# A hybrid decoder step on one core: the first row half's squares summed on VectorE, and query blocks without the learned rows' columns

## The chip, the cores and the metric

The kernel runs on one core of a Trainium2 chip. Its engines are TensorE (PE for its matmuls, PEld for its weight loads), VectorE (DVE), ScalarE (ACT), GpSimd (POOL) and SyncE (SP), whose queue issues most DMAs. The metric is the device time of one execution in microseconds. Lower is better.

## The reference, cut to what matters

512 prompt tokens, 8 sample tokens and 16 learned rows (meta tokens) of width 2048 pass through one layer: an input layer norm, one input projection (queries, keys, values, pool input), windowed attention and a multi-scale pooling side by side, an output projection, a layer norm, a gated feed-forward part of width 5632, and a layer norm. The learned rows stand at the front of the prompt as keys and values, and are dropped from the result. In short:

```python
h   = layer_norm(concat([meta, x]), ln_in_g, ln_in_b)
z   = h @ w_in + b_in                       # -> q | k | v | u
q,k = partial_rope(q, pos), partial_rope(k, pos)
mix = concat([window_attention(q, k, v, sinks), pool_mixer(u)]) @ w_o
h1  = layer_norm(alpha * h + mix, ln1_g, ln1_b)     # mean, mean of squared deviations
y   = layer_norm(alpha * h1 + (silu(h1 @ w_gate) * (h1 @ w_up)) @ w_down, ln2_g, ln2_b)
```

There is one layer, so nothing after the attention reads what the learned rows' own queries would give. All data are fp32.

## The kernel before, in words

Everything is held transposed: features on the 128 partitions, tokens along the free dimension. There are 536 columns: 16 learned rows (META), 8 sample tokens, 512 prompt tokens. They are worked on in two halves: in the input projection 276 columns (the learned rows and 260 tokens) and 260 columns; behind it, where the learned rows are gone, 260 and 260 (HN).

A product of fp32 accuracy is made of three single-pass products. `split` (lines 185 and 186) makes of a weight quarter of 512 columns a high half on ACT (a rounding copy) and a low half on DVE (the rest), into a ring of a few buffers; `products` (lines 201, 202, 204) then multiplies high by high, high by low and low by high. A block of 128 output features is `full_block`: 16 K tiles, in four quarters, each with three matmuls for each column half. The plain 32-bit matmuls (the mean, the variance, the products ahead) show as two instructions each.

The order of the work: input layer norm and keys and values (to about 90 us); eight query blocks (`q_block`) and eight pool blocks (`u_block`), interleaved with the attention of each query block by an explicit order on PE (to about 350 us); `out_proj(0)` for the first 260 columns, `out_proj(1)` for the second; then the layer norm of the second half with fourteen products computed ahead on plain 32-bit matmuls (to about 602 us); the gate and up products by a Strassen-Winograd scheme in 22 turns (to about 1490 us); the down products; the last layer norm.

`ln1(h, zs)` is the layer norm behind the output projection, a generator. For the first half it runs as the side of `out_proj(1)`: after each of the 16 feature blocks of that projection (each about 5.8 us of PE) one more piece of it is put into the program. Its steps: the mean by a matmul with a matrix of 1/2048; for each of eight pairs of K tiles (520 columns side by side) a subtraction of the mean on DVE (line 877), a square on ACT (line 879), and in `var` (line 873) two plain matmuls with the matrix of 1/2048 that add the pair's squares into one bank, which at the end holds the variance in all partitions. `rstd_of` (lines 234 to 240) makes the reciprocal root; then line 891 multiplies and line 894 scales, and `put` (856, 857) splits the result. The squares lie in a ring "t" of three buffers (NT), which also serves the loads of the residual (`hb`) and others; another ring "fill" of five (NF) is for the results of products computed ahead.

Inside these explicit orders, a planner places the instructions of each engine at build time by a simulated clock, by readiness and program order; the loads and splits of weights have a raised priority. Each engine then runs its list strictly in that order.

Of the kernel before, what the change touches and what calls it, by code (L numbers as in the profile page):

```python
# [7 lines left out]
F32 = mybir.dt.float32  # L8
F32R = mybir.dt.float32r
AF = mybir.ActivationFunctionType  # L10
# [3 lines left out]
P = 128  # L14
# [3 lines left out]
META = 16  # L18
# [5 lines left out]
HN = NTOK // 2  # L24
XN = META + HN
XH = [slice(0, XN), slice(XN, C_ALL)]
# [12 lines left out]
NF = 5  # L39
# [13 lines left out]
PG, PB, PBIAS, PSC, PG1, PB1, PSINK, PSS, NPAR = 0, 16, 32, 52, 60, 76, 92, 108, 110  # L53
# [13 lines left out]
def hybrid_step(ctx, tc, xin, w_in, w_o, w_g, w_u, w_d, w_pool, par_d, cst_d, ident_d, ln2gb, kct_d, vc_d, hist_d,  # L67
                ck_d, cv_d, sp_d, yp, ys, nkp, nvp, npp, nks, nvs, nps):
    nc = tc.nc
# [69 lines left out]
    par = cp.tile([P, NPAR], F32, name="par")  # L139
    onesd = cp.tile([P, P], F32, name="onesd")  # L140
# [34 lines left out]
    def load_raw(src, name):  # L175
        raw = wp.tile([P, 1024], F32, tag="raw", name=f"raw_{name}", bufs=NRAW)[:, :src.shape[-1]]
        with tc.high_priority(prio[0]):
            nc.sync.dma_start(raw, src)
        return raw

    def split(s, name, lo=None):

        wh, wl = [sp[0].tile(list(s.shape), F32R, tag=t, bufs=sp[1]) for t in ("wh", "wl")]
        with tc.high_priority(prio[0]):
            nc.scalar.copy(wh, s)  # L185
            last_lo[0] = (lo or nc.vector).tensor_sub(wl, s, wh.bitcast(F32)).ins  # L186
        return wh, wl
# [10 lines left out]
    def products(out, wh, wl, hi, lo, first, last, onto=False):  # L198

        for j, o in enumerate(out):  # L200
            nc.tensor.matmul(o, wh, hi[j], start=first, stop=False, skip_group_check=onto)  # L201
            nc.tensor.matmul(o, wh, lo[j], start=False, stop=False, skip_group_check=onto)  # L202
        for j, o in enumerate(out):
            nc.tensor.matmul(o, wl, hi[j], start=False, stop=last, skip_group_check=onto)  # L204

    def full_block(src, name, out, hi, lo, low=None, apart=False):


        def mm(w, g, js):
            for kk in range(4):  # L210
                k = g * 4 + kk
                sl = slice(kk * P, (kk + 1) * P)
                products([out[j] for j in js], w[0][:, sl], w[1][:, sl], [hi(k)[j] for j in js], [lo(k)[j] for j in js],
                         k == 0, k == KT - 1)

        js = list(range(len(out)))
        ws = []
        for h in range(2):
            raw = load_raw(src[:, h * 1024:(h + 1) * 1024], f"{name}_{h}")
            for g in range(2):  # L220
                ws.append(split(raw[:, g * 512:(g + 1) * 512], f"{name}_{h}{g}", low))
                mm(ws[-1], 2 * h + g, js[:1] if apart else js)
        if apart:
            for g in range(4):
                mm(ws[g], g, js[1:])
# [27 lines left out]
    with ExitStack() as sa:  # L253
# [3 lines left out]
        def mm_tile(name):  # L257
            return ps.tile([P, 512], F32, tag="mm", name=name, bufs=2)
# [4 lines left out]
        def zt_tile(name, n=C_ALL):  # L263
            return pa.tile([P, 2 * XN], F32, tag="zt", name=name, bufs=4)[:, :n]
# [80 lines left out]
        xw = [x.stop - x.start for x in XH]  # L345
        xhi = [act.tile([P, KT, xw[h]], F32R, name=f"xhi{h}") for h in range(2)]
        xlo = [act.tile([P, KT, xw[h]], F32R, name=f"xlo{h}") for h in range(2)]
# [32 lines left out]
                y = y[:, :, META:]  # L380
            last.append(nc.sync.dma_start(h_d[ks, :, HALF[h]].rearrange("k p c -> p k c"), y).ins)

        def in_block(i, name, halves=(0, 1), low=None, apart=False):
            out = [mm_tile(f"mm_{name}_{h}")[:, :xw[h]] for h in halves]
            full_block(w_in[i], name, out, lambda k: [xhi[h][:, k, :] for h in halves],
                       lambda k: [xlo[h][:, k, :] for h in halves], low, apart)
            return out

        def rope(z, dst, name):
            zs = zt_tile(f"zs_{name}")  # L390
            nc.vector.stream_shuffle(zs, z, SWAP)
            nc.vector.tensor_mul(zs, zs, rs)
            nc.vector.tensor_mul(z, z, rc)
            nc.vector.tensor_add(dst, z, zs)


        kT = pa.tile([P, 2, C_ALL], F32, name="kT")
# [16 lines left out]
        def kv_banks(h):  # L414
            return [mm_tile(f"kv{i}_{h}")[:, :xw[h]] for i in range(2)] + \
                   [aux_tile([P, 512], "sc", f"kv{i}_{h}", 4)[:, :xw[h]] for i in (2, 3)]
# [15 lines left out]
        out = kv_banks(0)  # L432
# [4 lines left out]
        for h in range(2):  # L437
# [27 lines left out]
            with step(*three):  # L465
                for i in range(4):
                    nc.scalar.activation(zkv[i][:, XH[h]], out[i], AF.Identity, bias=par[:, PBIAS + i:PBIAS + i + 1])
                if h == 0:
                    out = kv_banks(1)
                    x_split(1, 0)  # L470
        cst = pa.tile([P, NCST], F32, name="cst")
        rc, rs = cst[:, CC:CC + C_ALL], cst[:, CS:CS + C_ALL]
# [16 lines left out]
        for i in range(2):  # L489
            z = zkv[2 + i]  # L490
# [22 lines left out]
        nc.gpsimd.memset(qd, 0.0)  # L513

        def q_block(t):
            out = in_block(4 + t, f"q{t}")
            z = zt_tile(f"zq{t}")
            for h, o in enumerate(out):
                nc.vector.tensor_scalar(z[:, XH[h]], o, par[:, PBIAS + 4 + t:PBIAS + 5 + t], 0.125,
                                        op0=ALU.add, op1=ALU.mult)  # L520
            q = pa.tile([P, C_ALL], F32, tag="q", name=f"q{t}", bufs=3)
            rope(z, q, f"q{t}")
            for j in range(2):
                h = slice(64 * j, 64 * j + 64)
                nc.vector.tensor_copy(qd[h, j, t, :], q[h, C_S:C_P])
            return q
# [275 lines left out]
    pb, gp = Pool(fr), Pool(rr, Region("mid_b", F32R, MDW))  # L802
# [3 lines left out]
    def bank(name, w=HN):  # L806
        return ps.tile([P, 512], F32, tag="bank", name=name, bufs=banks)[:, :w]
# [17 lines left out]
    def pair(d, k2, h):  # L825
        return d[2 * k2:2 * k2 + 2, :, HALF[h]].rearrange("k p c -> p k c")

    def t_tile(name):
        return pb.tile([P, 2, HN], F32, tag="t", name=name, bufs=NT)
# [24 lines left out]
    def put(name, i, s):  # L854
        hi, lo = bop[name][i]
        nc.scalar.copy(hi, s)
        nc.vector.tensor_sub(lo, s, hi.bitcast(F32))

    def ln1(h, zs):


        mp = bank(f"mean{h}")
        nc.tensor.matmul(mp, onesd, zs, start=True, stop=True)
        mean = pb.tile([P, HN], F32, tag="zs", bufs=2)
        nc.scalar.copy(mean, mp)
        yield
        vp = bank(f"var{h}")
        both = lambda x: x.rearrange("p (a b) -> p a b", a=1).to_broadcast([P, 2, HN])
        sqs = []

        def var(k2):
            for j in range(2):
                nc.tensor.matmul(vp, onesd, sqs[k2][:, j, :], start=(k2 + j == 0), stop=(k2 + j == 8))

        for k2 in range(8):
            a = z1[h][k2]
            nc.vector.tensor_sub(a, a, both(mean))
            sqs.append(t_tile(f"sq{h}_{k2}"))
            nc.scalar.activation(sqs[k2], a, AF.Square)
            if k2:  # L880
                var(k2 - 1)
            if k2 % 2 and h == 0:
                yield
        var(7)
        with tc.high_priority(LP):
            r = rstd_of(pb, vp, P, f"ln1{h}")
        yield

        def norm(k2):
            a = z1[h][k2]  # L890
            nc.vector.tensor_mul(a, a, both(r))
            for j in range(2):
                k = 2 * k2 + j
                nc.scalar.activation(a[:, j, :], a[:, j, :], AF.Identity, scale=par[:, PG1 + k:PG1 + k + 1],
                                     bias=par[:, PB1 + k:PB1 + k + 1])
            nc.sync.dma_start(pair(h1_d, k2, h), a)
            return a

        if h == 0:
            for k2 in range(8):  # L900
                put("b11" if k2 < 4 else "b21", k2 % 4, norm(k2))
                yield
            return
        for i in range(4):
            c11, c21, c12 = z1[0][i], z1[0][i + 4], norm(i)
            c22 = norm(i + 4)
            yield

            t1, t2 = t_tile(f"t1_{i}"), t_tile(f"t2_{i}")
            nc.vector.tensor_sub(t1, c12, c11)  # L910
            nc.vector.tensor_sub(t2, c22, t1)
            put("t2", i, t2)
            put("t1", i, t1)
            yield
            t3, t4 = t_tile(f"t3_{i}"), t_tile(f"t4_{i}")
            nc.vector.tensor_sub(t3, c22, c12)
            put("t3", i, t3)
            nc.vector.tensor_sub(t4, c21, t2)
            put("t4", i, t4)
            put("b22", i, c22)  # L920
            yield
# [119 lines left out]
    def staged(go, i):  # L1041
# [17 lines left out]
        for n, y in ((1, go[1]), (3, t12), (5, t34)):  # L1059
# [6 lines left out]
            yield  # L1066

    g0 = ln1(0, out_proj(0))
    zs1 = out_proj(1, g0)
    for _ in g0:  # L1070
# [7 lines left out]
    for j, s in enumerate(sets[NKEEP:NKEEP + NFILL]):  # L1078
        if j % 2 == 0:
            f = pb.tile([P, 2, HN], F32, tag="fill", name=f"fill{j}", bufs=NF)  # L1080
# [27 lines left out]
    accp, rp, pb = Pool(fr), Pool(fr), Pool(fr)  # L1108
    low = fr.take(4 * 1280)
# [94 lines left out]
    for x, (c, j) in enumerate(pairs[2:], 2):  # L1204
# [5 lines left out]
        for i in range(5):  # L1210
# [7 lines left out]
            elif j == 0 and i == 0:  # L1218

                ah, al_ = [], []  # L1220
                for f in range(2 * len(PLAIN)):
                    t = slot(f"af{f}", (NTOK,), 16 + f).bitcast(F32)
# [19 lines left out]
    pb, zp = Pool(fr), Pool(Region("mid_c", F32, MDW))  # L1242
# [153 lines left out]
```

## Time and profile before

| | us |
|---|---|
| three runs | 1973.35, 1977.85, 1978.29 (median 1977.85) |
| the profiled execution | 1976.38, its span 1974.6 |
| busy in the span: PE, DVE, ACT | 1916.5, 1545.2, 936.6 |
| mean granted TensorE clock | 0.987 |

An engine's busy time is the union of its instructions' durations. PE's instructions overlap each other: a new one starts before the one ahead has ended, so the distance from start to start is what one costs in a dense stream. DMA is busy for about half of its capacity, and moves 162 GB/s over the span.

### The profile page before, as it was taken

What the parts mean: (1) busy time and instruction counts of PE and PEld (TensorE: products, weight loads), DVE (VectorE), ACT (ScalarE), POOL (GpSimd) and SP (SyncE); (2) the same over time, 40 slices, a digit from 0 to 9 for tenths busy, and PEclk for the clock granted to TensorE, in tenths of its full rate; (3) what the DMA queues carried; (4) which work ended last, traced back from release to release, by engine and by line L of the source; (5) the groups of instructions that cost most, each with busy time, mean ns of one, the idle gap of its engine ahead of it and who ended that gap; (6) DMA issues with size and microseconds to landing.
All of it is one profiled execution on the core that took longest, in us unless ns stands there. A gap on an engine that the chain in (4) does not pass through costs nothing.

```text
span 1974.6 us, 39350 instructions
## 1 busy us (share of the span) xinstructions
PE 1916.5 (97%) x15571; PEld 1881.8 (95%) x15571; DVE 1545.2 (78%) x2730; ACT 936.6 (47%) x1805; POOL 2.5 (0%) x8
## 2 busy tenths in 40 slices
PE   8999999999999999999999999999999999999995
PEld 8999999999988888999999999999999999999995
DVE  6665657766776878788888888888777888888878
ACT  6644445545654434455554545555545434344331
POOL 0000000000000000000000000000000000000000
PEclk9999999999999999999999999999999999999997
DMA  8732222665744453545445453545549664645332
GB/s 264 231 101 67 67 81 71 216 201 170 247 151 145 136 174 125 171 136 167 145 140 162 148 169 125 169 143 169 176 173 365 209 223 166 223 168 202 86 97 87
DMA packets 144984, 319.25 MB, mean 162 GB/s; under 512 B 14160, under 2 KB 65944, under 8 KB 144696
## 3 DMA queue, kind: packets, MB, share of 16 engines
q1 hardware_dynamic: 143680, 314.65, 48.2%
q8 instruction: 122, 2.00, 0.4%
q10 hardware_dynamic: 1120, 2.10, 0.3%
q14 instruction: 62, 0.51, 0.1%
HBM read 265.20 MB, written 54.03 MB: 162 GB/s over the span
## 4 chain that ended last, share of the span: by engine, by line
PE 58%; DVE 5%; DMA 2%; issue 1%; ACT 1%; DVEq 0%; ACTq 0%; SPq 0%
PE tri L201 7%; PE tri L204 7%; PE tri L202 7%; PE p_u L201 6%; PE p_u L202 6%; PE p_u L204 6%; PE p_g L201 6%; PE p_g L204 6%; PE p_g L202 6%; DMA fr<-in_w_g_dram 2%; DVE fr L194 2%; DVE rr L186 1%; PE d L204 1%; DMA t_d<-fr 1%; PE d L202 1%
## 5 line engine op out<-in xcount | busy, mean ns | idle before, releaser
L185 ACT CAST rr<-fr 128x512 fp32r<-128x512 f32 (+1 forms) x1056 | 655.6, 643 | 849.7 <-DVE fr L194 289.0
L186 DVE TENSOR_TENSOR rr<-fr,rr 128x512 fp32r<-128x512 f32 (+1 forms) x1056 | 733.4, 716 | 265.6 <-ACT rr L185 253.7
L194 DVE TENSOR_TENSOR fr<-fr 128x1024 f32<-128x1024 f32 (+1 forms) x304 | 319.3, 1050 | 37.3 <-DMA fr<-in_w_g_dram 21.7
L201 PE MATMUL p_g<-rr 128*128 128x260 f32 x800 | 231.2, 290 | 15.9 <-DVE fr L999 6.7
L204 PE MATMUL p_g<-rr 128*128 128x260 f32 x800 | 225.8, 287 | 1.1 <-DVE rr L186 1.1
L201 PE MATMUL p_u<-rr 128*128 128x260 f32 x800 | 225.5, 283 | 0.0
L204 PE MATMUL p_u<-rr 128*128 128x260 f32 x800 | 222.0, 282 | 0.0
L202 PE MATMUL p_g<-rr 128*128 128x260 f32 x768 | 219.6, 287 | 0.0
L202 PE MATMUL p_u<-rr 128*128 128x260 f32 x768 | 216.0, 282 | 0.0
L204 PE MATMUL tri<-rr 128*128 128x260 f32 x696 | 196.8, 283 | 1.2 <-DVE rr L186 1.2
L201 PE MATMUL tri<-rr 128*128 128x260 f32 x696 | 197.1, 283 | 0.8 <-ACT rr L185 0.8
L202 PE MATMUL tri<-rr 128*128 128x260 f32 x696 | 196.7, 283 | 0.0
L201 PEld LDWEIGHTS p_g<-rr 128*128 128x128 f32 x800 | 154.2, 193 | 19.9 <-DVE fr L999 7.7
L204 PEld LDWEIGHTS p_g<-rr 128*128 128x128 f32 x800 | 153.3, 193 | 1.4 <-DVE rr L186 1.3
L201 PEld LDWEIGHTS p_u<-rr 128*128 128x128 f32 x800 | 150.6, 188 | 0.0
L204 PEld LDWEIGHTS p_u<-rr 128*128 128x128 f32 x800 | 149.7, 189 | 0.0
L202 PEld LDWEIGHTS p_g<-rr 128*128 128x128 f32 x768 | 148.0, 193 | 0.0
L201 PE MATMUL o<-rr 128*128 128x260 f32 x512 | 146.0, 286 | 0.3 <-ACT rr L185 0.3
L202 PEld LDWEIGHTS p_u<-rr 128*128 128x128 f32 x768 | 144.3, 188 | 0.0
L204 PE MATMUL o<-rr 128*128 128x260 f32 x512 | 143.9, 283 | 0.2 <-DVE rr L186 0.2
L202 PE MATMUL o<-rr 128*128 128x260 f32 x512 | 144.0, 282 | 0.0
L204 PEld LDWEIGHTS tri<-rr 128*128 128x128 f32 x696 | 131.3, 189 | 1.7 <-DVE rr L186 1.4
(299 smaller groups left out, 4591.5 us busy)
## 6 DMA issues: line engine op xcount, KB each, us to landing
fr<-in_w_g_dram SPq DMA_DIRECT2D x95, 512.0 KB
fr<-in_w_u_dram SPq DMA_DIRECT2D x95, 512.0 KB
fr<-in_w_d_dram SPq DMA_DIRECT2D x64, 640.0 KB
t_d<-fr SPq DMA_DIRECT2D x140, 260.0 KB
fr<-in_w_o_dram SPq DMA_DIRECT2D x64, 512.0 KB
fr<-in_w_in_dram SPq DMA_DIRECT2D x46, 512.0 KB
rr<-t_d SPq DMA_DIRECT2D x87, 260.0 KB
mid_b<-t_d SPq DMA_DIRECT2D x53, 260.0 KB
```

Of the source, the lines that this page charges most:

```text
L185: nc.scalar.copy(wh, s)
L186: last_lo[0] = (lo or nc.vector).tensor_sub(wl, s, wh.bitcast(F32)).ins
L194: i = op(*args).ins
L201: nc.tensor.matmul(o, wh, hi[j], start=first, stop=False, skip_group_check=onto)
L202: nc.tensor.matmul(o, wh, lo[j], start=False, stop=False, skip_group_check=onto)
L204: nc.tensor.matmul(o, wl, hi[j], start=False, stop=last, skip_group_check=onto)
```

## The change

Two things. First, the query blocks compute only the 520 columns of tokens, not those of the 16 learned rows: the first column half of a query block's matmuls goes from 276 to 260 columns, and the steps behind it (bias and scale, rotation) are made on 520 instead of 536. Pool blocks are as before.

Second, in the layer norm of the first row half the eight pairs' squares are no longer sent to PE one by one. DVE adds them up into one buffer `ss`, which takes the first place of the ring "fill", and two plain matmuls over that sum stand in for sixteen. The pieces of the generator (where it yields) are the same. The second row half is as before.

```diff
-        def in_block(i, name, halves=(0, 1), low=None, apart=False):
-            out = [mm_tile(f"mm_{name}_{h}")[:, :xw[h]] for h in halves]
-            full_block(w_in[i], name, out, lambda k: [xhi[h][:, k, :] for h in halves],
-                       lambda k: [xlo[h][:, k, :] for h in halves], low, apart)
+        def in_block(i, name, c0=0, apart=False):
+
+            halves, cs = (0, 1), (slice(c0, xw[0]), slice(0, xw[1]))
+            out = [mm_tile(f"mm_{name}_{h}")[:, cs[h]] for h in halves]
+            full_block(w_in[i], name, out, lambda k: [xhi[h][:, k, cs[h]] for h in halves],
+                       lambda k: [xlo[h][:, k, cs[h]] for h in halves], apart=apart)
...
-        def rope(z, dst, name):
-            zs = zt_tile(f"zs_{name}")
+        def rope(z, dst, name, c0=0):
+            zs = zt_tile(f"zs_{name}")[:, c0:]
+            z = z[:, c0:]
             nc.vector.stream_shuffle(zs, z, SWAP)
-            nc.vector.tensor_mul(zs, zs, rs)
-            nc.vector.tensor_mul(z, z, rc)
-            nc.vector.tensor_add(dst, z, zs)
+            nc.vector.tensor_mul(zs, zs, rs[:, c0:])
+            nc.vector.tensor_mul(z, z, rc[:, c0:])
+            nc.vector.tensor_add(dst[:, c0:], z, zs)
...
-            out = in_block(4 + t, f"q{t}")
+            out = in_block(4 + t, f"q{t}", META)
...
-                nc.vector.tensor_scalar(z[:, XH[h]], o, par[:, PBIAS + 4 + t:PBIAS + 5 + t], 0.125,
+                nc.vector.tensor_scalar(z[:, (slice(META, XN), XH[1])[h]], o, par[:, PBIAS + 4 + t:PBIAS + 5 + t], 0.125,
...
-            rope(z, q, f"q{t}")
+            rope(z, q, f"q{t}", META)
...
             nc.vector.tensor_sub(a, a, both(mean))
+            if h == 0:
+
+                if k2 == 0:
+                    ss = pb.tile([P, 2, HN], F32, tag="fill", name="ss", bufs=NF)
+                    nc.scalar.activation(ss, a, AF.Square)
+                else:
+                    sq = t_tile(f"sq{h}_{k2}")
+                    nc.scalar.activation(sq, a, AF.Square)
+                    nc.vector.tensor_add(ss, ss, sq)
+                if k2 % 2:
+                    yield
+                continue
             sqs.append(t_tile(f"sq{h}_{k2}"))
             nc.scalar.activation(sqs[k2], a, AF.Square)
             if k2:
                 var(k2 - 1)
-            if k2 % 2 and h == 0:
-                yield
-        var(7)
+        if h == 0:
+            for j in range(2):
+                nc.tensor.matmul(vp, onesd, ss[:, j, :], start=(j == 0), stop=(j == 1))
+        else:
+            var(7)
```

## Rows read from the trace of the kernel before

**Rows 1.** The page: busy time by engine, and the granted clock in 40 slices.
```profile
PE 1916.5 (97%) x15571; PEld 1881.8 (95%) x15571; DVE 1545.2 (78%) x2730; ACT 936.6 (47%) x1805; POOL 2.5 (0%) x8
PEclk9999999999999999999999999999999999999997
```

**Rows 2.** What PE waited for from 100 to 560 us: total, times, longest.
```profile
PE o L201 <- ACT rr L185: 0.3, 1, 0.3
```

**Rows 3.** By stretch: length, busy PE, PEld, DVE, ACT, POOL; granted clock; DMA.
```profile
100.00:150.00 50.00, 50.00 (x421) 48.08 (x421) 33.11 (x106) 20.97 (x58) 0.00 (x0) 1.00 0.29 96
300.00:310.00 10.00, 10.00 (x66) 9.57 (x63) 8.89 (x38) 5.29 (x22) 0.00 (x0) 0.72 0.49 153
451.00:487.00 36.00, 36.00 (x275) 35.00 (x274) 22.50 (x40) 18.13 (x31) 0.00 (x0) 1.00 0.51 162
```

**Rows 4.** PE in order of time (start, us, instruction) in a query block.
```profile
150.72 0.29 PE L201 MATMUL mm_q<-rr 128*128 128x276 f32 x1
150.85 0.29 PE L202 MATMUL mm_q<-rr 128*128 128x276 f32 x1
150.98 0.29 PE L201 MATMUL mm_q<-rr 128*128 128x260 f32 x1
151.10 0.28 PE L202 MATMUL mm_q<-rr 128*128 128x260 f32 x1
...
155.18 0.29 PE L201 MATMUL mm_q<-rr 128*128 128x276 f32 x1
```

**Rows 5.** PE in order of time in the output projection of the second half.
```profile
488.31 0.28 PE L204 MATMUL o<-rr 128*128 128x260 f32 x1
...
495.51 0.28 PE L204 MATMUL o<-rr 128*128 128x260 f32 x1
```

**Rows 6.** PE in order of time around one pair of the variance, and later.
```profile
456.85 0.28 PE L204 MATMUL o<-rr 128*128 128x260 f32 x1
456.97 1.04 PE L873 MATMUL var<-fr 128*128 128x260 f32 x4
...
457.97 0.28 PE L202 MATMUL o<-rr 128*128 128x260 f32 x1
...
460.65 0.28 PE L204 MATMUL o<-rr 128*128 128x260 f32 x1
```

**Rows 7.** DVE, then ACT, in order of time, with idle time ahead and its releaser.
```profile
452.25 4.96 DVE L877 TENSOR_TENSOR fr<-fr 128x520 f32<-128x520 f32 x8
457.13 1.89 DVE L186 TENSOR_TENSOR rr<-fr,rr 128x512 fp32r<-128x512 f32 x3
...
462.58 0.69 DVE L186 TENSOR_TENSOR rr<-fr,rr 128x512 fp32r<-128x512 f32 x1 [1.68 <-ACT rr L185]
...
452.74 0.62 ACT L185 CAST rr<-fr 128x512 fp32r<-128x512 f32 x1 [0.94 <-PE o L202]
...
458.10 0.64 ACT L879 ACTIVATE fr<-fr 128x520 f32<-128x520 f32 x1 [0.39 <-PE var L873]
```

**Rows 8.** DVE from 452 to 512 us, one group: busy us, mean ns, idle.
```profile
L891 DVE TENSOR_TENSOR fr<-fr 128x520 f32<-128x520 f32 x8 | 5.0, 692 | 0.0
```

**Rows 9.** PE in order of time: a wait; around the products computed ahead.
```profile
508.30 0.39 PE L204 MATMUL o<-rr 128*128 128x260 f32 x1 [0.22 <-DVE rr L186]
...
545.69 1.92 PE L963 MATMUL p_g<-fr 128*128 128x260 f32 x8
...
602.45 0.48 PE L201 MATMUL p_g<-mid_b,rr 128*128 128x260 f32 x1
```

**Rows 10.** What PE waited for from 600 to 1400 us: total, times, longest.
```profile
PE p_g L201 <- ACT rr L185: 7.4, 10, 1.7
PE p_g L201 <- DVE fr L999: 6.7, 5, 1.4
PE p_g L201 <- DVE fr L1009: 4.1, 3, 2.9
PE p_g L204 <- DVE rr L186: 2.8, 6, 1.1
```

## Prediction

> **What bounds the kernel now.** I read the page first: PE is busy for 97% of the span, at a granted clock near full in every slice, with DVE at 78% and ACT at 47% [rows 1]. A busy PE need not be a full PE, so the second view is what PE waits for between 100 and 560 us, the stretch that holds the query blocks, the output projection and the first layer norm: two waits, the longer 0.3 us [rows 2], the other shorter. The third is the table by stretch: in 100 to 150 us (query and pool blocks) and 451 to 487 us (the projection with the first half's norm) PE is busy for the whole stretch at clock 1.00, while DVE has 34% and 38% of it free [rows 3]. So both edits lie where PE is the bound and nothing else is. There, a PE instruction taken out shortens the run by its slot in the stream (start to next start), not by its printed duration: the 0.28 us of a matmul are pipelined, and the starts are 0.12 us apart [rows 4, 5].
>
> **Query blocks without the 16 learned columns.** Eight blocks, each 16 K tiles, each K tile six matmuls: three on 276 columns and three on 260. The change makes the first three 260 wide: 8 x 16 x 3 = 384 matmuls lose 16 columns. The slots: from 150.72 to 155.18 us the stream goes through six K tiles, 4.46 us, so 0.743 us for one [rows 4]. At 260 columns throughout, 60 matmuls of the output projection take from 488.31 to 495.51 us, 0.120 us each, so six take 0.720 us [rows 5]. The difference, 0.023 us by 128 K tiles, is **2.9 us**. A check from below: at the 2.4 GHz that a granted clock of 1.00 stands for, 16 columns by 384 are 2.6 us. I take 2.9. On DVE the five steps of a block on these columns (bias, shuffle, three of the rotation) lose 16 of 536 columns too. At the pace of a 520 column step, 692 ns [rows 8], that is 21 ns for each of 40 steps, 0.9 us on an engine that is not the bound. Priced at nothing; were DVE the gate there, it would be a further gain. Nothing waits longer: the learned rows' queries had no reader in the scores, whose queries start behind them. The weights of the blocks are loaded as before, by the same DMAs.
>
> The Trainium skill, "TensorE: Matmul & The Clock Gate", section "Back-to-back issue gap", speaks against this size: it holds that in a stream of weight load and matmul pairs the spacing is set by both, some 81 ns at 128 columns and 131 ns at 512, so that 16 columns would be worth only about 2 ns (an estimate from those two figures), 0.8 us in all. The trace does not bear it out here: the wide matmuls start 0.13 us before the next and the narrow ones 0.12 us, in one stream with equal weight tiles [rows 4].
>
> **Squares summed on DVE.** Before, each of the eight pairs of K tiles of the first half sends two 32-bit matmuls over its squares, and each shows as two instructions. One pair's four instructions push the output projection back: without them the matmul after the one at 456.85 would end its second step at 457.09 us, but that second step starts at 457.97 [rows 6], so 0.88 us a pair. One pair stays (the two matmuls over the sum), seven go: 7 x 0.88 = **6.2 us** off PE, in a stretch where PE does not wait.
>
> Added: seven additions of 128x520 on DVE. The nearest rows are 692 ns each as records, or 4.96 us for a run of eight, 0.62 us each end to end [rows 7, 8]. So 4.3 to 4.8 us of DVE. DVE is busy for 22.5 of the 36 us from 451 to 487 [rows 3]; the stretch shrinks to some 30 us and DVE rises to about 27 of it. On average it still fits, with 3 us to spare. The eight squares stay on ACT, their first now in a buffer of the ring that the later fills use; that ring's first later use is after 546 us, long after the sum is read, so no price.
>
> The added wait: an addition waits for its square (about 0.64 us of ACT), and behind it on DVE stand the subtractions that make the low weight halves (L186), for which PE's third product waits. How much can PE bear? A high half begins when PE frees the oldest of five buffers [rows 7], so four quarters of twelve matmuls, 4 x 1.44 = 5.8 us, lie ahead of it; less 0.62 us for the high half and 0.69 for the low one, the quiet margin is some 4.5 us. The planner already puts eight mean subtractions in one run at 452.25; the low half behind them (its high half was begun at 452.74) ends near 457.8, and its quarter, counted in order, is first used at 460.65: 2.8 us of margin left [rows 6, 7]. Of that margin 1.76 us are two groups of variance matmuls (the one of [rows 6] and one more before 460.65), which delay PE and which the change removes. So about 1.0 us of margin remains before any addition. If all seven additions (4.3 us) stood ahead of the same subtraction, PE would wait 3.3 us; if they come behind it, into the 1.68 us hole at 462 and those after it [rows 7], nothing. An addition needs its square, and the squares share ACT with the high halves: the third stood at 458.10 [rows 7]. So most additions come late: I take **0.3 us** of 0 to 3.3. The last matmuls wait for one more step than before (square, then addition): 0 to 1.3 us if the planner puts them early on PE, taken as **0.3 us**. The reciprocal root starts up to 0.7 us later in its place, hidden: PE's first instructions on the normalised half stand at 545.69 us or later [rows 9].
>
> In exchange ACT loses a wait: its third square waited for a variance matmul to free a buffer (0.39 us at 458.10, [rows 7]); now the addition frees it. Off the bound, nothing.
>
> **What is late next.** After this comes the dense run of eight multiplications and the splits of the normalised half, which already leaves PE a short wait at 508.30 us (0.22 us, [rows 9]); it is not touched, and stays. Behind 602 us the gate and up products only start earlier.
>
> **The sum.** 2.9 + 6.2 - 0.3 - 0.3 = 8.5 us. The profiled execution took 1976.4 us (span 1974.6): 1976.4 - 8.5 = **1967.9 us**. That execution is 1.5 us under the median of the three runs, 1977.85, which themselves spread over 4.9 us; 0.3%, about what a measurement of this kernel can tell from no change, is 5.9 us.
>
> **The rivals.**
> *DVE becomes the gate for some microseconds.* The burst above at its worst, 3.3 us of PE waiting, and 1.3 us at the last matmuls: 9.1 - 4.6 = 4.5 us of gain, **1971.9 us**. For it: the margin of 1.0 us, and a planner that does put eight equal steps in one run. Against it: additions that wait for ACT one by one. Chance 0.18.
> *The slot of a query matmul is the weight load's.* Weight loads fill 95% of the span [rows 1]; if they and not the columns set the slots, the query part gives nothing: 6.2 - 0.6 = 5.6 us of gain, **1970.8 us**. Against it stand the unequal starts in [rows 4]. Chance 0.03. (The page named above points this way.)
> *The gain is lost behind both edits.* Between 300 and 310 us, among the small products of the sample attention, the granted clock averages 0.72: 2.8 us of full clock [rows 3]. If work that arrives 3 us sooner falls otherwise, a dip of this size can come twice or not at all; a second one together with half of the burst leaves 9.1 - 2.8 - 2.3 = 4.0 us of gain, **1972.4 us**. Chance 0.11.
> *Slower.* The gate and up products that use results computed ahead already make PE wait, 7.4 + 6.7 + 4.1 + 2.8 = 21 us, for ACT and DVE in an order that the planner chose [rows 10]. The edits do not touch them, but the planner orders from its own clock, which the edits move. If its new order doubles those waits, 1967.9 + 21 = **1988.9 us**; it is slower by more than 0.3% once they grow by over 14.4 us, two thirds. For it: these waits are many (24) and short. Against it: they come from a fixed set of extra additions, and PE has a stretch of 32-bit matmuls, from 545.69 to 602.45 us, in front [rows 9], in which a displacement of DVE is worked off. Chance 0.08.
> *The change does not do what it says*, for example because the planner still lets the projection wait at the same point for DVE: no gain, 1976.4. Chance 0.02.
>
> **How the numbers follow.** Forecast 0.58, rivals 0.18, 0.03, 0.11, 0.08, 0.02. Faster by over 0.3% needs less than 1971.9 by the median: the forecast, the weight loads' case and about half of the first rival, together 0.70, less a little for runs that lie 2 us apart: 0.66. Slower 0.08. Same 0.26. The range: the whole gain of 9.1 us, on a run as far under the profiled one as the lowest of before (3.0 us), 1964.3; upward to the rival that loses its gain behind the edits, 1972.4, with 2.6 us, half the spread of the runs: 1975. Outside it lie slower and part of the rest, under 2 in 10.
>
> **What would show it.** Right: the starts of query matmuls all 0.12 us apart and each K tile 0.72 us; four instead of 32 variance instructions of the first half; seven additions of about 0.69 us on DVE between 450 and 480 us; the first product computed ahead, at 545.69 us now, starting 8 to 9 us earlier; the rest of the span unchanged in length. Wrong: waits of PE for L186 or for the sum between 440 and 480 us of more than 1 us (first rival); a K tile still over 0.735 us (the spacing); or an equal early start at the products ahead, with more than 21 us of waits behind 602 us (slower).

## The result

The changed kernel took 1963.6 us (median of six runs, 1961.83 to 1966.66), the kernel before beside it 1975.98 us (six runs, 1972.70 to 1978.53). The ratio is 0.9941, with a 95% interval of 0.9930 to 0.9953, so 9 to 14 us less, some 11.7 us. Two more sets of the same program gave 0.9944 (0.9930 to 0.9957) and 0.9937 (0.9923 to 0.9951). Beside the last set two runs of the kernel before, at 2083 and 2658 us with a mean granted clock of 0.846 and 0.652, are left out. The forecast was 1967.9 us, 8.5 us less: the sign and the size hold, the gain came out about 3 us larger.

The profiled execution took 1966.66 us, span 1964.8. The page's first line, to be read against [rows 1]:

```profile
PE 1908.0 (97%) x15543; PEld 1874.5 (95%) x15543; DVE 1548.5 (79%) x2737; ACT 936.6 (48%) x1805; POOL 2.5 (0%) x8
```

PE has 28 instructions fewer (the seven pairs), DVE seven more, ACT as many as before. What follows are the lines of the changed kernel that answer to [rows 4], [rows 6] and [rows 9]: PE in order of time in a query block, at the one variance group that is left, and at the products computed ahead.

```profile
150.61 0.29 PE L201 MATMUL mm_q<-rr 128*128 128x260 f32 x1
150.74 0.28 PE L202 MATMUL mm_q<-rr 128*128 128x260 f32 x1
150.85 0.28 PE L201 MATMUL mm_q<-rr 128*128 128x260 f32 x1
150.97 0.28 PE L202 MATMUL mm_q<-rr 128*128 128x260 f32 x1
...
154.97 0.28 PE L201 MATMUL mm_q<-rr 128*128 128x260 f32 x1
...
478.36 0.28 PE L204 MATMUL o<-rr 128*128 128x260 f32 x1
478.48 1.04 PE L899 MATMUL var<-fr 128*128 128x260 f32 x4
...
479.48 0.28 PE L202 MATMUL o<-rr 128*128 128x260 f32 x1
...
500.66 0.39 PE L204 MATMUL o<-rr 128*128 128x260 f32 x1 [0.22 <-DVE rr L186]
...
538.05 1.92 PE L980 MATMUL p_g<-fr 128*128 128x260 f32 x8
...
594.82 0.48 PE L201 MATMUL p_g<-mid_b,rr 128*128 128x260 f32 x1
```

Six K tiles of a query block go from 150.61 to 154.97 us, 0.727 us each, where [rows 4] had 0.743. The busy time of all 768 query matmuls, before and then in the changed kernel (length of the stretch, busy PE, PEld and DVE of these instructions alone, granted clock of the stretch, DMA):

```profile
86.60:351.59 264.99, 97.13 (x768) 95.23 (x768) 7.21 (x16) 0.99 0.28 91
...
88.30:350.22 261.92, 94.67 (x768) 92.92 (x768) 7.08 (x16) 0.99 0.29 96
```

That is 2.46 us less, and the same to 0.01 us in the second profile of before and in the other two of the changed kernel. No query matmul ran at the lower clock in any of these five profiles.

One variance group of four instructions costs its 0.88 us (478.60, where the second step would stand without it, to 479.48), and it is the only one of the first half. The short wait of 0.22 us that [rows 9] showed at 508.30 stands unchanged at 500.66. The first product computed ahead starts at 538.05 instead of 545.69, 7.6 us earlier, and 9.3 us earlier when counted from the first query matmul.

What PE waited for from 100 to 553 us in the changed kernel (total, times, longest; compare [rows 2]):

```profile
PE o L201 <- ACT rr L185: 0.3, 1, 0.3
PE o L204 <- DVE rr L186: 0.2, 1, 0.2
```

The kernel before has the same two lines, 0.5 us together. There is no wait for the sum and none new for the low halves.

DVE around the mean subtractions (compare [rows 7]), then PE at the first use of the low half that comes behind them, then the stretch from 451 to 481 us by engine (columns as in [rows 3]):

```profile
450.77 4.96 DVE L880 TENSOR_TENSOR fr<-fr 128x520 f32<-128x520 f32 x8
455.66 0.68 DVE L186 TENSOR_TENSOR rr<-fr,rr 128x512 fp32r<-128x512 f32 x1
456.26 0.69 DVE L889 TENSOR_TENSOR fr<-fr 128x520 f32<-128x520 f32 x1
...
472.63 0.69 DVE L889 TENSOR_TENSOR fr<-fr 128x520 f32<-128x520 f32 x1
...
457.41 0.28 PE L204 MATMUL o<-rr 128*128 128x260 f32 x1
...
451.00:481.00 30.00, 30.00 (x249) 29.88 (x249) 25.77 (x47) 18.57 (x31) 0.00 (x0) 1.00 0.62 198
```

The low half behind the run of eight ends at 456.34 and is used at 457.41: 1.07 us of margin. The first addition stands behind it, the last ends at 473.32, 5.2 us before PE asks for the sum at 478.48. DVE is busy for 25.8 of these 30 us.

The span cut at the first PE instruction of each part, in us (two profiles of before, three of the changed kernel; each row begins where the one above ends):

| stretch | before | before again | changed | again | third |
|---|---|---|---|---|---|
| start to first query matmul | 86.64 | 87.99 | 88.34 | 87.44 | 87.85 |
| to first of the output projection | 264.95 | 264.91 | 261.89 | 260.42 | 261.83 |
| to first product ahead | 194.10 | 194.10 | 187.83 | 188.07 | 187.87 |
| to first gate product | 56.76 | 56.77 | 56.77 | 56.77 | 56.77 |
| to first down product | 885.75 | 884.80 | 883.55 | 882.34 | 882.52 |
| to the end | 486.40 | 486.45 | 486.48 | 486.38 | 486.30 |

Means of the spans: 1974.8 before, 1963.1 changed, 11.7 us apart, as the ratio has it. Between profiles with 6.8 us at half clock in the query stretch, that stretch gives 3.06 us (264.95 to 261.89; the 260.42 of one profile has only 3.4 us at half clock). 2.46 of the 3.06 us are the query matmuls'. The other 0.6 us go with the place where the lower clock fell: on pool matmuls at 304 us before (their starts to next starts sum to 98.6 us, 96.0 without it), on attention matmuls at 343 us in the changed kernel. The projection stretch gives 6.2 us, the gate and up turns some 2.5 us.

### The profile page after: what moved, and what is told of

Same layout as the page of the kernel before. It is cut to its first block, busy times and chain, and to the rows that moved or that the text cites. A ratio compares the mean times of both kernels' runs of the same rounds, so it can differ in the third digit from the quotient of the medians.

```text
span 1964.8 us, 39296 instructions
## 1 busy us (share of the span) xinstructions
PE 1908.0 (97%) x15543; PEld 1874.5 (95%) x15543; DVE 1548.5 (79%) x2737; ACT 936.6 (48%) x1805; POOL 2.5 (0%) x8
```

## The experiments

**Each edit alone.** The first kernel has the narrower query blocks, and `ln1` as before:

```diff
-            if h == 0:
...
-                continue
             sqs.append(t_tile(f"sq{h}_{k2}"))
             nc.scalar.activation(sqs[k2], a, AF.Square)
             if k2:
                 var(k2 - 1)
+            if k2 % 2 and h == 0:
+                yield
-        if h == 0:
-            for j in range(2):
-                nc.tensor.matmul(vp, onesd, ss[:, j, :], start=(j == 0), stop=(j == 1))
-        else:
-            var(7)
+        var(7)
```

> The query blocks without the 16 learned columns alone; the squares go to PE pair by pair as before. Theory (the two edits add up, each worth its PE slots): the stretch from the first query matmul to the first matmul of the output projection is 3 us shorter than before, the time 2.9 us (1.5 to 4.5) less, ratio about 0.9985. Rival (the whole program's order moved, and the 2.2 us gained behind 602 us come from that): a gain of 5 us or more from this edit alone. Rival (slots set by the weight loads): no gain.

Measured: 0.9977 (0.9962 to 0.9993), 1971.74 us. The query stretch goes from 85.91 to 346.36 us, 260.45 us, the shorter form that the changed kernel shows too when less of it runs at the lower clock; the projection stretch is 193.97 us, as before.

The second has the sum on DVE, and the query blocks with 276 columns.

> The sum of the squares on DVE alone; the query blocks keep 276 columns. Theory (the two edits add up): the stretch from the first matmul of the output projection to the first product computed ahead is 6.2 us shorter (194.1 to 187.9), the time 6.2 us less (4.5 to 8.5), ratio about 0.9969, and PE waits no more than before in that stretch. Rival (DVE as the gate): 3 us of new waits for L186 there and a gain of about 3 us.

Measured: 0.9960 (0.9948 to 0.9973), 1968.16 us. The projection stretch by its two ends, PE in order of time:

```profile
351.95 0.36 PE L201 MATMUL o<-rr 128*128 128x260 f32 x1
...
539.90 1.91 PE L977 MATMUL p_g<-fr 128*128 128x260 f32 x8
```

187.95 us, against 194.10; the query stretch is 264.94 us. So in its own stretch each edit is worth its slots, 6.2 us and 2.5 us (the query matmuls' own), and neither touches the other's. The totals, 4.5 and 7.9 us, are each about 2 us above the slots, within their intervals. Part of that may lie where neither edit is: the gate and up turns are 880.14 and 880.75 us long in these two profiles, where before has 885.75 and 884.80. In both kernels 288 of PE's 7314 instructions there stand elsewhere than before. Both profiles are the fastest run of their kernel.

**The same programs again.** No edit.

> The changed kernel unchanged, for a second profile and the granted clock of every run. Theory (the 2 us by which runs of one program differ, and the 2.2 us gained behind 602 us, are stretches at half clock that fall on dense or on waiting PE): the program's order being the same, the lengths of its stretches differ by multiples of about 1.7 us (half of 3.41 us) where a stretch at half clock falls, and not by less; the times of the runs fall as the mean granted clock rises, 1.7 us for 0.0009 of the clock. Rival (the planner's order behind 602 us differs from before and is worth 2.2 us): the stretch from 594.8 us to the first down product comes out at 883.5 us again, within 0.3.

> The kernel before, unchanged, as a null comparison and for a second profile. Theory (the 2 to 3 us of gain over the slots of both edits are stretches at half clock that fall by chance): ratio 1.000 within its interval, the stretch from the first gate product to the first down product 881 to 886 us with 10 to 17 us at half clock, as in the profiles of the changed kernel. Rival (the changed kernel has fewer such stretches there, as a consequence of the edits): 17 us at half clock again, and 885.7 us.

> The changed kernel once more, beside the kernel before in both places. Theory (9.2 us of slots, the rest chance): ratio 0.9953 by the slots alone, 0.994 to 0.996; the query stretch 3.06 us and the projection stretch 6.2 us shorter than in the profile of before taken here, after 1.7 us for each 3.41 us at half clock in them. Rival (something behind 602 us belongs to the edits): 0.994 or less and a gate and up stretch shorter by 2 us at equal time at half clock.

Measured: the changed kernel 0.9944 and 0.9937 as told above; the kernel before against itself 0.9994 (0.9983 to 1.0004). The stretches stand in the table. Two things come apart there. The query stretch moves by 1.5 us between profiles of one program, with the clock at its end: the changed kernel's first profile, then its second, in the stretch from 340 to 350 us (the eighth value is the granted clock):

```profile
340.00:350.00 10.00, 10.00 (x113) 7.77 (x112) 10.00 (x35) 6.64 (x18) 0.00 (x0) 0.67 0.75 238
...
340.00:350.00 10.00, 10.00 (x138) 8.66 (x136) 10.00 (x36) 6.43 (x17) 0.00 (x0) 1.00 0.74 232
```

This is chance: the same instructions, at 0.67 in the one and at full clock in the other (in the first, the dip of [rows 3] at 300 us has moved here).

The gate and up turns, though, are 884.8 and 885.8 us in both profiles of before and 882.3 to 883.6 in all three of the changed kernel. My theory had put these 2.5 us down to the clock. The time at half clock does not make them: these turns have 17.1 and 10.2 us at half clock before, and 17.1, 13.7 and 13.7 in the changed kernel. With half of that taken off (an estimate) 877.2 and 879.7 us are left before, 875.0, 875.5 and 875.7 in the changed kernel. That points to the program, but it is not shown: the two profiles of before are 2.5 us apart by this measure themselves. Nor did either reading come out to the letter, as the changed kernel's lengths are neither all within 0.3 us of each other nor multiples of 1.7 us apart. The second profile of before, 884.8 us with 10.2 at half clock, still fits what my theory gave for it.

The order of instructions does differ a little: from the first product ahead to the first down product, 3 of DVE's 1217 and 4 of ACT's 901 instructions stand elsewhere than before, at 658 to 665, 773 and 1423 to 1429 us, in code that the edits do not touch; two profiles of one program show no difference. And what PE waits for there, in the changed kernel:

```profile
PE p_g L201 <- ACT rr L185: 6.8, 9, 1.7
PE p_g L201 <- DVE fr L1016: 6.7, 5, 1.4
PE p_g L201 <- DVE fr L1026: 3.5, 3, 2.5
PE p_g L204 <- DVE rr L186: 2.9, 6, 0.9
```

19.9 us (20.0 and 19.4 in the other two profiles), against 21.0 in [rows 10] (22.0 in the second profile of before). That is 1 to 3 us less waiting, which goes the way of the 2.5 us. That the few moved instructions make all of it was not tried: the planner's order can't be set by itself.

**How much room DVE has.** Each of the seven additions three times:

```diff
-                    nc.vector.tensor_add(ss, ss, sq)
+                    for _ in range(3):
+                        nc.vector.tensor_add(ss, ss, sq)
```

> The changed kernel with each of the seven additions made three times, 14 more of them (the variance then is not the reference's). Theory (DVE has about 3 us of room in that stretch and a margin of some microseconds, then it is the gate): DVE needs 22.5 + 21 x 0.62 = 35.5 us in the 30 us of the stretch; 4.5 us of that are margin, so PE waits for L186 1 to 6 us, and the stretch from the first matmul of the output projection to the first product computed ahead is 189 to 194 us instead of 187.8. Rival (DVE is nowhere near the gate): 187.8 to 188.2.

Measured: 1.0013 (1.0004 to 1.0022), 1978.19 us, and the projection stretch is 201.40 us: 13.6 us more than in the changed kernel for 8.7 us of additions, outside what I expected. DVE and PE in order of time, what PE waited for from 340 to 620 us, and the stretch from 480 to 500 us:

```profile
479.46 0.43 DVE L846 SCALAR_TENSOR_TENSOR fr<-fr,o 128x260 f32<-128x260 f32 x1 [1.58 <-DMA fr<-h_d]
...
483.24 5.18 DVE L890 TENSOR_TENSOR fr<-fr 128x520 f32<-128x520 f32 x7
...
488.47 2.10 PE L900 MATMUL var<-fr 128*128 128x260 f32 x4 [9.60 <-DVE fr L890]
...
PE var L900 <- DVE fr L890: 9.6, 1, 9.6
PE o L204 <- DVE rr L186: 1.2, 2, 1.0
...
480.00:500.00 20.00, 11.53 (x77) 11.14 (x78) 15.61 (x27) 6.11 (x10) 0.00 (x0) 0.74 0.28 86
```

DVE is the gate here, but at another place than the first rival had it. The low halves cost PE 1.2 us in all; the sum costs it 9.6 us, because its last seven additions end at 488.4 while PE, strictly in order, has stood before the two matmuls over it since 478.9. The granted clock averages 0.74 over the 20 us around that wait. PE, back at work at 488.5, ran its first 4.0 us at half of the clock, which is 2.0 of the remaining 2.8 us; the other 0.8 us are open. The sum is ready 15 us later than in the changed kernel, for 8.7 us of additions: other steps stand in front of the last seven, and DVE itself waited 1.6 us for a load at 479 us. So the change has 5.2 us of room before its reader, and 8.7 us of further DVE work are more than that room and the gaps hold.

**The second half's squares too.** First in place: the sum on DVE for both halves, nothing else.

```diff
-            if h == 0:
...
+            if k2 == 0:
+                ss = pb.tile([P, 2, HN], F32, tag="fill", name=f"ss{h}", bufs=NF)
+                nc.scalar.activation(ss, a, AF.Square)
+            else:
+                sq = t_tile(f"sq{h}_{k2}")
+                nc.scalar.activation(sq, a, AF.Square)
+                nc.vector.tensor_add(ss, ss, sq)
...
```

> The changed kernel with the second half's squares summed on DVE too, but no product moved: the two matmuls over the sum stand on PE behind the first product computed ahead. Theory (a sum on DVE needs PE work ahead of its reader): PE waits 5 to 9 us for the sum behind 540 us, which eats the 6.2 us of slots; 1962 to 1967 us. Rival (the gain of the kernel with both halves comes from the sum alone): about 1952 us, no wait over 1 us there.

Measured: 0.9980 (0.9970 to 0.9990), 1971.48 us, some 7 us slower than the changed kernel, and outside the 1962 to 1967 us that I expected. Then with two of the products computed ahead put in front of the second sum's matmuls:

```diff
+        if h == 1:
+            yield
...
-    for f in (fills[0], g1, fills[0], g1):
+    for f in (fills[0], g1, fills[0], g1, fills[1], fills[1], fills[2], fills[2], g1):
...
-    for j, f in enumerate(fills[1:]):
+    for j, f in enumerate(fills[3:], 2):
```

> The changed kernel, with the second half's squares summed on DVE too: two instead of sixteen plain matmuls, put behind two further products computed ahead so that PE has work while the sum is made. Theory (a plain matmul taken out of a dense PE stretch is worth its slots): 14 x 2 x 0.22 = 6.2 us less than the changed kernel, about 1957.5 us. Rival (DVE has no more room there: it is busy for 42.6 of 57 us, and with 4.8 us more for 47 of 51): the first gate product waits for the second half's operands and the gain is 0 to 3 us.

> The kernel with both halves' squares summed on DVE and two products moved ahead of the second sum, once more, for its time beside the others and a second profile. Theory: about 1951 us; the waits of PE in the gate and up turns about 14 us, at most two stretches at half clock among them.

Measured: 0.9875 (0.9858 to 0.9893) and 0.9887 (0.9874 to 0.9901), 1951.76 and 1951.90 us: 12 us under the changed kernel, and 6 us under what the slots had let me expect. PE at the second sum, in place and then with two products in front:

```profile
551.74 2.10 PE L891 MATMUL var<-fr 128*128 128x260 f32 x4 [9.16 <-DVE fr L887]
...
552.44 1.15 PE L893 MATMUL var<-fr 128*128 128x260 f32 x4 [2.15 <-DVE fr L887]
```

In place PE waits 9.2 us for the sum, more than the 6.2 us of slots that it saves. The stretch from the first product ahead to the first gate product is 62.50 us, 5.7 us longer: 3.0 us of that is wait less slots, the rest PE work at half of the clock behind the wait (last section), for which the expectation had no term. With 7 us of products in front the wait is 2.15 us, and the stretch from the first product ahead to the first gate product goes from 56.77 to 52.64 us, which is 6.2 less 2.1. That explains 4 of the 12 us. The gate and up turns are 867.5 and 872.8 us in the two profiles, with 13.3 and 15.7 us of waits (about 14 were expected) and 3.4 and 10.2 us at half clock: one program, 5 us apart. For the rest, the new order without the second sum (the same `yield`, ahead of `var(7)`, and the same two loops):

> The changed kernel with the order of the second half's norm as in the kernel with both halves summed on DVE (two further products computed ahead in front of the last step of the variance, and the later pieces of the norm put two products later), but the second half's squares on PE as in the changed kernel: 32 variance instructions, of which two pairs... the last pair stands behind the two products. Theory (of the 12 us that kernel is under the changed one 6.2 are PE slots and the rest comes from the order): 6 us under the changed kernel, about 1958 us, with fewer than 14 us of waits in the gate and up turns. Rival (the whole 12 us come from the sum): 1964 us and 20 us of waits there.

Measured: 0.9903 (0.9888 to 0.9918), 1955.18 us, by the ratios 7 to 8 us under the changed kernel (0.9903 against 0.9937 to 0.9944). The order alone carries most of it: the stretch to the first gate product is 56.76 us, as before, and the gate and up turns are 873.85 instead of 883.55, of which some 3.4 us are less time at half clock (10.2 instead of 17.1 us). What PE waited for there:

```profile
PE p_u L201 <- ACT rr L185: 9.8, 6, 2.8
PE p_u L201 <- DVE fr L1027: 2.6, 1, 2.6
PE p_g L201 <- DVE fr L1017: 1.3, 2, 0.9
```

The waits sit in other places (before the up products instead of the gate products) and sum to less, 15.8 us (fewer than 14 were expected); 183 of DVE's and 81 of ACT's instructions there are in another order than in the changed kernel. What makes this order better was not followed further. Last, three products in front:

> Both halves' squares summed on DVE, with three instead of two products moved ahead of the second sum. Theory (the sum is ready 2.2 us after PE asks for it, and a product takes 3.5 us): the wait of 2.2 us at the second sum goes, and the time is 2 us under the one with two products, about 1950 us. Rival (the norm that now starts 1.3 us later delays the first gate product): 1952 us or more, with a new wait behind 590 us.

Measured: 0.9899 (0.9881 to 0.9917), 1957.65 us, where about 1950 was expected; by the ratios that is 2 to 5 us more than with two products, and the intervals overlap. The wait at the sum went, and the stretch to the first gate product fell by another 2.4 us, to 50.22; but the gate and up turns went back to 879.60 us, with 20.3 us of waits and 6.8 us at half clock. The local theory held; behind it the profile shows a new order, and more lost there than won here.

## Why the prediction was right, point by point

**What bounds the kernel.** PE in both stretches, as read: PE work that was taken out came back slot for slot, and no wait grew.

**The query blocks.** 2.9 us forecast, 2.46 us found in the query matmuls themselves. The mechanism held: fewer columns made shorter slots. The size was 0.4 us too large, because the pace after the change, 0.720 us for a K tile, was taken from the output projection; the narrower query blocks take 0.727. The 2.6 us of the "check from below" was closer, but not below. That the stretch as a whole gave 3.06 us, nearer to the forecast, was luck in where the lower clock fell. The weight loads' case is out. By the Trainium skill, "TensorE: Matmul & The Clock Gate", section "Back-to-back issue gap", the estimate was 0.8 us; the measurement is 2.46.

**The squares.** 6.2 us forecast, 6.2 us found (194.10 to 187.83; 187.95 with this edit alone).

**The two costs.** 0.3 us for the burst and 0.3 us at the last matmuls were forecast; neither was paid. The margin behind the eight subtractions was worked out as 1.0 us and is 1.07. The additions all came behind that point, and the sum was ready 5.2 us before PE reached its reader.

**The sum.** 8.7 us by slots and no costs, where the forecast had 9.1 less 0.6, 8.5: two small errors that nearly cancel. The whole gain is larger, 11.7 us, and the median of 1963.6 us lies 0.7 us below the low end of the range, 1964.3. The step that missed is "the rest of the span unchanged in length": the gate and up turns got some 2.5 us shorter, and about 1 us more of the mean of the query stretch is clock. I had put the planner's new order among the rivals with a loss alone, and as a doubling of waits. In the profiles those turns changed with the other sign, with a few instructions moved; that the order makes the 2.5 us is likely and not shown.

**The rivals.** *DVE as the gate* did not come about, and its mechanism was put at the wrong place: with three times the additions PE waits at the sum's reader (9.6 us), not for the low halves (1.2 us). *A second dip of the clock*: none in the three profiles of the changed kernel; the dip moved from 300 to 340 us in two of them and was half as long in the third. Such a dip does come and go, though: three experiments with the same query blocks (the tripled additions, the sum in place, the second profile with both sums) have 10.2 us at half clock there, and a query stretch of 263.62 us. *Slower*: no; but in the experiments the planner's order behind an edit was worth some 6 us beyond the clock (883.55 to 873.85 us with the products moved), so its weight was not too large.

## What to carry to other kernels

In a stretch where PE never waits, an instruction is worth its start to start distance, and here that sum held to half a microsecond; the distance after the change should come from the same kind of block. Moving such work to an engine with free time is safe as long as the result is ready before the in-order engine reaches its reader: the room is the distance from the last step of the new chain to that reader (5.2 us here; 9.2 us short in the second half), and it is made by putting other work in front of the reader. Where a planner orders the program, leave room in the forecast, with either sign, for places that the edit does not touch.

## What the runs showed of the hardware that was not expected

Two long waits of PE cost more than their length. The granted clock around them, first at the tripled additions and then at the second sum in place (columns as in [rows 3]):

```profile
482.50:492.30 9.80, 3.83 (x13) 3.44 (x14) 6.07 (x10) 1.83 (x2) 0.00 (x0) 0.50 0.19 60
492.70:500.00 7.30, 7.30 (x63) 7.30 (x63) 7.04 (x12) 3.90 (x8) 0.00 (x0) 1.00 0.40 125
...
547.50:557.30 9.80, 5.56 (x13) 4.36 (x14) 6.47 (x10) 2.35 (x5) 0.00 (x0) 0.50 0.00 0
```

In the first PE stood from 478.9 to 488.5 us, and the clock was at its lower level (1.2 of 2.4 GHz) from 482.5 to 492.3; 9.6 us of wait and 1.2 us more made a stretch 13.6 us longer. In the second PE stood from 542.6 to 551.7 us, and 5.6 us of its work behind the wait ran at the lower level, some 2.8 us of loss. The wait of 2.15 us with two products in front had no lower clock near it in either profile.

Runs of one program differ along with their mean granted clock: of the kernel before 19 runs at 0.987 average 1976.9 us, 17 at 0.988 average 1975.6 and 10 at 0.989 average 1974.3; the three at 0.990 average 1975.1. From 0.987 to 0.989 that is 1.3 us for each 0.001, where I had expected 1.9 of the changed kernel.
